# A Strassen pair's last two products moved behind the next pair's first two, with weight blocks in quarter buffers and stores on ScalarE

## The chip, the cores and the metric

The kernel runs on one core of a Trainium2 chip. The metric is the device time of one execution in microseconds (us), the median of the runs shown. TensorE (PE in the profile) multiplies into PSUM, VectorE (DVE) and ScalarE (ACT) read PSUM and work on SBUF, GpSimd (POOL) works on SBUF alone, and SyncE (SP) does nothing here but issue DMAs. Each of these engines executes its own list of instructions in order, so one that waits holds up all that stand behind it on its engine.

## The reference, cut to what matters

One decoder layer over a sequence of 2048 positions and 1024 channels, in float32:

```python
h = rms_norm(x, g_norm) * (1 + scale) + shift          # scale, shift from silu(c) @ w_mod
proj = h @ w_in                                        # (2048, 1024) @ (1024, 8192)
x_rnn, z_rnn, q, k, v, z_attn, g_r, g_a = split(proj)  # eight parts, 1024 wide each
y_rnn  = (rg_lru(conv4(x_rnn)) * silu(z_rnn)) @ w_out_rnn      # two sigmoid gates by 8 blocks 128x128
y_attn = (dilated_attention(rope(q), rope(k), v) * silu(z_attn)) @ w_out_attn
merged = sigmoid(g_r + b_r) * y_rnn + sigmoid(g_a + b_a) * y_attn
out = rms_norm(x + gate * (merged @ w_o), g_final)
```

The change concerns `proj`. All of it but the part `v` is computed by the loop that the change rearranges.

## The kernel before, in words

**Precision.** Each float32 operand is split into a high part and the rest (`hi_act` on ScalarE, then `lo_pool` on GpSimd, lines 150 to 157), and a product is three matmuls (`mm3`, line 145).

**Two halves.** The sequence is cut in four banks of 512 positions. A half (`f` = 0, 1) takes two banks. In each half `values_half` computes `v` from 256-wide weight blocks (`load_wv`, `values`), and builds the right-hand operands B11, B21 (`build_even`), B12, B22 and their sums T1 to T4 (`build_odd`): transposes on TensorE into the PSUM pool `pg`, evicted by ScalarE and VectorE. Then come 28 *pairs*: 20 in the stage of the recurrence and the gates (8 of `recurrent`, 12 of `gate_pairs`), and 8 of `qk_pairs`.

**A pair** (`strassen`, line 240) computes two 128-row blocks of `proj` (i = 0, 1) for the half's two banks (j = 0, 1) with seven products instead of eight, Strassen's scheme in Winograd's form. A product is 4 x 3 = 12 matmuls of 512 columns, so a pair is 84. Four PSUM accumulators take them, each a bank of the pool `pj`: X (B11, later B21), Z (T2), W (T3, later T4) and V (T1, later B22). Before the second product of an accumulator may start, its first contents are read out: u1 = X by ScalarE, u2 = Z + u1 (line 260) and u3 = W + u2 (line 265) by VectorE, and V + u3 for the block (1, 1) by `done`, through `total` (line 282).

**The left operands** of the seven products come from the weights. In the first half `load_raw` (line 185) fetches one pair's block of 1024 x 256 into a single buffer `wraw`, as one DMA or several; `left_operands` forms sums of its quarters a11, a12, a21, a22 on VectorE (s1 and s2 at lines 218, 219 and 226, a21 in place at line 221) in the single buffers `s1` and `s2`, and `split_s` splits each operand into one of seven buffers `S`. Each S is also stored to memory (`sD`, line 231) and in the second half `stored_operands` (line 234) fetches it back instead. All these DMAs are issued by SyncE.

**Consumers** (`done`): a recurrent pair's x blocks go through a convolution (line 530), a split (xh, xl), the two gate products into the pool `pg` (line 539) and a chain of element-wise steps to a scan (lines 540 to 553). Gates and q, k are scaled or rotated and stored.

**Order.** No order is written by hand in this part: a scheduler places every instruction of every engine by priority, which goes by the order of the program, and by when it expects its inputs. DMAs take eight completion semaphores in turn, and one waits for the DMA before it on the same semaphore where that isn't known to have landed. The attention after it, 1566 us into the span and later, is scheduled by hand and isn't touched.

Of the kernel before, what the change touches and what calls it, by code (L numbers as in the profile page):

```python
# [10 lines left out]
F32 = mybir.dt.float32  # L11
F32R = mybir.dt.float32r
BF16 = mybir.dt.bfloat16
I32 = mybir.dt.int32
AF = mybir.ActivationFunctionType
ALU = mybir.AluOpType
AX = mybir.AxisListType
PSUM = bass.MemoryType.PSUM
DRAM = bass.MemoryType.DRAM

P = 128
# [63 lines left out]
def decoder_block(ctx, tc, x, c, positions, g_norm, w_mod, b_mod, w_in, b_gate, conv_w, conv_b,  # L85
# [4 lines left out]
    def T(pool, shape, dt, tag, **kw):  # L90
        cnt[0] += 1
        return pool.tile(shape, dt, tag=tag, name=f"{tag}_{cnt[0]}", **kw)
# [57 lines left out]
    def hi_act(o, i):  # L150
        nc.scalar.activation(o, i, AF.Copy)  # L151
# [4 lines left out]
    def lo_pool(o, i, h):  # L156
        nc.gpsimd.tensor_tensor(o, i, h.bitcast(F32), ALU.subtract)  # L157
# [24 lines left out]
        nc.sync.dma_start(raw[:], src.rearrange("(k p) m -> p k m", p=P))  # L182
        return split_w(raw[:], lo)

    def load_raw(pieces):

        raw = T(wq, [P, KT, 2 * P], F32, "wraw", bufs=1)
        a = 0
        for src in pieces:
            n = src.shape[1]  # L190
            nc.sync.dma_start(raw[:, :, a : a + n], src.rearrange("(k p) m -> p k m", p=P))  # L191
            a += n
        assert a == 2 * P
        return raw

# [4 lines left out]

    def split_s(src):
        t = T(wq, [P, 2, KH, P], F32R, "S", bufs=7)
        hi_act(t[:, 0], src)
        lo_pool(t[:, 1], src, t[:, 0])
        return t

    n_pair = [0, 0]

    def left_operands(raw):

        a11, a12 = raw[:, :KH, :P], raw[:, KH:, :P]
        a21, a22 = raw[:, :KH, P:], raw[:, KH:, P:]
        yield split_s(a11)
        s1 = T(wq, [P, KH, P], F32, "s1", bufs=1)
        s2 = T(wq, [P, KH, P], F32, "s2", bufs=1)
        nc.vector.tensor_tensor(s1[:], a21, a22, ALU.add)
        nc.vector.tensor_tensor(s2[:], s1[:], a11, ALU.subtract)
        yield split_s(s2[:])  # L220
        nc.vector.tensor_tensor(a21, a11, a21, ALU.subtract)
        yield split_s(a21)
        yield split_s(s1[:])
        yield split_s(a12)
        yield split_s(a22)
        nc.vector.tensor_tensor(s2[:], a12, s2[:], ALU.subtract)
        yield split_s(s2[:])

    def first_operands(x, pieces):
        for i, t in enumerate(left_operands(load_raw(pieces))):  # L230
            nc.sync.dma_start(sD[7 * x + i], t[:].bitcast(F32))
            yield t

    def stored_operands(x):
# [5 lines left out]
    def strassen(up, f, pieces, done):  # L240

        x, n_pair[f] = n_pair[f], n_pair[f] + 1
        ops = stored_operands(x) if f else first_operands(x, pieces)

        def prod(ps, b, first, last):
            s = next(ops)
            bh, bl = B[b]
            for k in range(KH):
                mm3(ps[:], s[:, 0, k, :], s[:, 1, k, :], bh[:, k, :], bl[:, k, :],
                    first=first and k == 0, last=last and k == KH - 1, skip_group_check=True)  # L250

        X = T(pj, [P, CH], F32, "pj")
        prod(X, "B11", True, False)
        Z = T(pj, [P, CH], F32, "pj")
        prod(Z, "T2", True, True)
        u1 = T(up, [P, CH], F32, "u1", bufs=1)
        u2 = T(up, [P, CH], F32, "u2", bufs=2)
        with tc.high_priority():
            nc.scalar.activation(u1[:], X[:], AF.Copy)
            nc.vector.tensor_tensor(u2[:], Z[:], u1[:], ALU.add)  # L260
        W = T(pj, [P, CH], F32, "pj")
        prod(W, "T3", True, False)
        u3 = T(up, [P, CH], F32, "u3", bufs=1)
        with tc.high_priority():
            nc.vector.tensor_tensor(u3[:], W[:], u2[:], ALU.add)  # L265
        V = T(pj, [P, CH], F32, "pj")
        prod(V, "T1", True, False)
        done(1, 1, V, u3)
        prod(X, "B21", False, True)
        done(0, 0, X, None)  # L270
        prod(W, "T4", False, True)
        done(1, 0, W, u2)
        prod(V, "B22", False, True)
        done(0, 1, V, u2)

    def total(dst, ps, u, perm=lambda ap: ap):

# [4 lines left out]
                nc.vector.tensor_tensor(dst, perm(ps[:]), perm(u[:]), ALU.add)  # L282

    def load_wv(m):
        raw = load_raw([wcol(4 * D + m * 2 * P, 2 * P)])
        ws = []
        for k in range(0, KT, KH):
            wh = T(wq, [P, KH, 2 * P], F32R, "S", bufs=7)
            wl = T(wq, [P, KH, 2 * P], F32R, "S", bufs=7)
            hi_act(wh[:], raw[:, k : k + KH, :])  # L290
            lo_pool(wl[:], raw[:, k : k + KH, :], wh[:])
            ws.append((wh, wl))
        return ws

# [3 lines left out]
    def wcol(c0, n=P):  # L298
        return w_in[0, :, c0 : c0 + n]
# [11 lines left out]


    wq = pools.open("wq", side="right", bufs=1)
    pj = pools.open("pj", bufs=5, space=PSUM)
    pg = pools.open("pg", bufs=3, space=PSUM)
    vx = pools.open("vx", bufs=1)

    xv = x[0].rearrange("(n j r) d -> n r j d", n=NB, r=4)
# [175 lines left out]
    def reset_rows(rp, f):  # L494
        bigr = T(rp, [P, HALF], BF16, "bigr")
        for q in range(2):
            t = T(rp, [P, CH], I32, "posi", bufs=1)
            n = 2 * f + q
            nc.sync.dma_start(t[:], positions[0:1, n * CH : (n + 1) * CH].broadcast_to([P, CH]))
            nc.vector.tensor_scalar(bigr[:, q * CH : (q + 1) * CH], t[:], 0, BIG, ALU.is_equal, ALU.mult)  # L500
        return bigr

    def recurrent(rp, bigr, f, m):
        raw = T(rp, [P, 2, P], F32, "gr_", bufs=1)
        nc.sync.dma_start(raw[:, 0, :], w_a[0, m])
        nc.sync.dma_start(raw[:, 1, :], w_x[0, m])
        gh = T(rp, [P, 2, P], F32R, "gh", bufs=2)
        gl = T(rp, [P, 2, P], F32R, "gl", bufs=2)
        hi_act(gh[:], raw[:])
        lo_pool(gl[:], raw[:], gh[:])  # L510
        cw = lambda j: par[:, C_CW + 8 * j + m : C_CW + 8 * j + m + 1]
# [101 lines left out]

    def qk_pairs(qp, f, Ct, St):
        for base, dstT, qs in ((2 * D, qT, -SCALE), (3 * D, kT, 1.0)):
            def scaled(t, ps, u):
                if u is None:
                    nc.scalar.activation(t[:], ps[:], AF.Copy, scale=qs)
                else:
                    total(t[:], ps, u)  # L620
                    if qs != 1.0:
                        nc.scalar.activation(t[:], t[:], AF.Copy, scale=qs)

            def rotated(i, j, ps, u):
                n = 2 * f + j
                cq = slice(j * CH, (j + 1) * CH)
                t0 = T(qp, [P, CH], F32, "t0", bufs=3)
                t1 = T(qp, [P, CH], F32, "t1", bufs=2)
                scaled(t0, ps, u)
                nc.vector.stream_shuffle(t1[:], t0[:], swap)  # L630
                nc.gpsimd.tensor_tensor(t0[:], t0[:], Ct[:, cq], ALU.mult)
                nc.vector.tensor_tensor(t1[:], t1[:], St[:, cq], ALU.mult)
                nc.vector.tensor_tensor(t1[:], t1[:], t0[:], ALU.add)
                for hh in range(4):
                    r0 = (4 * i + hh) * P
                    nc.sync.dma_start(dstT[r0 : r0 + 32, :, n * P : (n + 1) * P],
                                      t1[hh * 32 : (hh + 1) * 32, :].rearrange("p (r j) -> p r j", r=4))

            strassen(qp, f, [wcol(base + hh * P, 32) for hh in range(H)], rotated)
            cuts = []  # L640
            for t in range(6):
                pieces = []
                i0 = t * P
                while i0 < (t + 1) * P:
                    hd, i = divmod(i0, 96)
                    n = min(96 - i, (t + 1) * P - i0)
                    pieces.append((i0 - t * P, hd * P + 32 + i, n))
                    i0 += n
                cuts.append(pieces)
            for t in range(0, 6, 2):  # L650
                def plain(i, j, ps, u):
                    n = 2 * f + j
                    t0 = T(qp, [P, CH], F32, "t0", bufs=3)
                    scaled(t0, ps, u)
                    for p0, r0, m in cuts[t + i]:
                        nc.sync.dma_start(dstT[r0 : r0 + m, :, n * P : (n + 1) * P],
                                          t0[p0 : p0 + m, :].rearrange("p (r j) -> p r j", r=4))

                strassen(qp, f, [wcol(base + r0, n) for pc in cuts[t : t + 2] for _, r0, n in pc], plain)


    def gate_pairs(ep, f):
        for m in range(0, KT, 2):
            for base, dst, b0 in ((5 * D, zaT, None), (6 * D, grT, C_BG), (7 * D, gaT, C_BG + 8)):
                def gate(i, j, ps, u):
                    n = 2 * f + j
                    t = T(ep, [P, CH], F32, "ev", bufs=3)
                    v = ps
# [33 lines left out]
    for f in range(2):  # L702
# [16 lines left out]
                next(gates, None)  # L719
        for _ in gates:  # L720
            pass
        pools.close("rp")
        qp = pools.open("qp", bufs=1)
        tabs = rotary_tables(qp, f)
# [2 lines left out]
        else:  # L727
            xp = pools.open("xp", side="right", bufs=1)
            x0 = load_x(xp, 2, "x", 2)
            norm_x(xp, x0, 1)  # L730
        qk_pairs(qp, f, *tabs)
        pools.close("qp")
    pools.close("wq", "hp", "pg", "pj")
    wp[0] = pools.open("wp", side="right", bufs=1)
# [573 lines left out]
```

## Time and profile before

| | us |
|---|---|
| median of 3 runs (2512.85 to 2521.59) | 2516.35 |
| the profiled execution, its own time | 2514.89 |
| its span, first to last instruction | 2513.1 |
| PE, DVE, ACT, POOL busy | 2306.7, 1409.9, 1174.5, 1027.6 |
| mean granted TensorE clock | 0.969 |

The profiled execution is 1.5 us below the median. In it the first half's values and builds run up to 166 us, its recurrence and gates to about 645, its rotary tables and q, k pairs to 861; the second half's values run to 980, its pairs to 1565. A group of rows has the source line, the engine, the operation, output and inputs, the shapes and the count, then busy time and mean duration, then the engine's idle time just before and what ended it. The waits are rows of the form "who waited <- for whom", total, times, longest.

### The profile page before, as it was taken

Reading aid. Unit: us, or ns where it says so; the run is one execution under the profiler, and the core shown is the slowest. Engines: PE = TensorE matmul, PEld = TensorE weight load, DVE = VectorE, ACT = ScalarE, POOL = GpSimd, SP = SyncE. Lnnn points to the kernel's source line nnn. Section 1 sums busy time; section 2 is a strip of 40 time slices with the busy share of each in tenths; the row PEclk is TensorE's granted clock in tenths of the full one; section 3 lists DMA queues with packets and bytes.
Section 4 is the critical chain, followed back from the end, with each engine's and each line's share of the span. In section 5 each row is a group of like instructions: output and inputs, shape, how many; then the busy total and the mean of one; then the engine's idle time right before and its main releaser. Section 6 shows DMA issues by size and latency. Waiting matters only on the chain.

```text
span 2513.1 us, 34056 instructions
## 1 busy us (share of the span) xinstructions
PE 2306.7 (92%) x11653; PEld 1920.7 (76%) x11653; DVE 1409.9 (56%) x2479; ACT 1174.5 (47%) x2216; POOL 1027.6 (41%) x793
## 2 busy tenths in 40 slices
PE   5898998989978889999999999899999898979998
PEld 5886776766756788888888777688878787868887
DVE  7917565656664381544435442466666767756533
ACT  2425555555522342645446110566667666633211
POOL 2547555655434452211111010466676757552100
PEclk9999999999989899999999999899999999989999
DMA  7256666666868726667666876677677677677652
GB/s 239 81 176 240 232 229 231 228 234 218 263 191 230 237 85 207 214 219 238 208 221 208 273 227 203 192 201 216 182 211 212 183 199 214 184 220 243 204 167 92
DMA packets 426181, 518.39 MB, mean 206 GB/s; under 512 B 67486, under 2 KB 310294, under 8 KB 424984
## 3 DMA queue, kind: packets, MB, share of 16 engines
q1 hardware_dynamic: 426008, 516.21, 65.1%
q8 instruction: 92, 1.51, 0.2%
q14 instruction: 81, 0.66, 0.1%
HBM read 321.07 MB, written 195.04 MB: 205 GB/s over the span
## 4 chain that ended last, share of the span: by engine, by line
PE 49%; DVE 12%; DMA 11%; issue 6%; ACT 5%; POOL 4%; SPq 3%; DVEq 0%; POOLq 0%; ACTq 0%
PE pj L143 34%; PE pq L143 7%; DMA wraw<-in_w_in_dram 5%; PE o L143 2%; PE sc L143 2%; POOL S L157 2%; PE pg L143 1%; DMA yraw<-yaT 1%; DVE wl L160 1%; ACT S L151 1%; PE pT L899 1%; ACT wh L151 1%; SPq L191 1%; PE sc L1009 1%; PE pT L919 1%
## 5 line engine op out<-in xcount | busy, mean ns | idle before, releaser
L143 PE MATMUL pj<-T,S 128*128 128x512 f32 x4704 | 1144.7, 403 | 55.9 <-DVE u L265 21.4
L143 PEld LDWEIGHTS pj<-T,S 128*128 128x128 f32 x4704 | 896.3, 192 | 289.8 <-DVE u L265 26.6
L157 POOL TENSOR_TENSOR S<-wraw,S 128x512 fp32r<-128x512 f32 (+1 forms) x140 | 229.9, 1650 | 284.7 <-ACT S L151 230.2
L143 PE MATMUL pj<-yh,wh 128*128 128x512 f32 x512 | 218.2, 427 | 18.1 <-ACT yh L151 15.9
L143 PE MATMUL pj<-yh,wl 128*128 128x512 f32 x512 | 204.7, 400 | 1.7 <-DVE wl L160 1.7
L143 PE MATMUL pj<-yl,wh 128*128 128x512 f32 x512 | 205.1, 401 | 1.1 <-POOL yl L157 1.0
L151 ACT ACTIVATE S<-wraw 128x512 fp32r<-128x512 f32 (+1 forms) x140 | 97.5, 709 | 161.1 <-DMA wraw<-in_w_in_dram 143.1
L143 PE MATMUL pj<-S,T 128*128 128x256 f32 x1152 | 158.0, 295 | 15.1 <-POOL S L157 8.0
L143 PEld LDWEIGHTS pj<-S,T 128*128 128x128 f32 x1152 | 150.1, 201 | 18.5 <-POOL S L157 9.5
L157 POOL TENSOR_TENSOR S<-s,S 128x512 fp32r<-128x512 f32 x84 | 125.6, 1495 | 71.9 <-ACT S L151 67.9
L160 DVE TENSOR_TENSOR wl<-wraw,wh 128x1024 fp32r<-128x1024 f32 x64 | 94.2, 1472 | 69.2 <-ACT wh L151 67.9
L530 DVE SCALAR_TENSOR_TENSOR xc<-xr,par,xc 128x512 f32<-128x512 f32 x96 | 93.9, 978 | 66.8 <-ACT xc L528 66.3
L143 PEld LDWEIGHTS pj<-yh,wh 128*128 128x128 f32 x512 | 98.7, 193 | 31.5 <-ACT yh L151 17.5
L519 POOL TENSOR_TENSOR zs<-zs,sg 128x512 f32<-128x512 f32 x32 | 42.5, 1328 | 182.9 <-ACT sg L518 169.4
L143 PEld LDWEIGHTS pj<-yh,wl 128*128 128x128 f32 x512 | 97.9, 191 | 24.8 <-DVE wl L160 3.1
L157 POOL TENSOR_TENSOR yl<-yraw,yh 128x512 fp32r<-128x512 f32 x40 | 57.2, 1437 | 144.3 <-ACT yh L151 136.6
L157 POOL TENSOR_TENSOR kq<-kraw,kq 128x512 fp32r<-128x512 f32 (+1 forms) x64 | 101.6, 1590 | 27.2 <-ACT kq L151 23.9
L260 DVE TENSOR_TENSOR u<-pj,u 128x512 f32<-128x512 f32 x56 | 38.5, 687 | 130.8 <-PE pj L143 125.5
L143 PEld LDWEIGHTS pj<-yl,wh 128*128 128x128 f32 x512 | 98.8, 193 | 14.4 <-POOL yl L157 3.1
L830 ACT ACTIVATE pp<-pp,st 128x128 f32<-128x128 f32 (+3 forms) x128 | 71.4, 559 | 80.8 <-DVE st L829 78.9
L143 PE MATMUL pq<-oh,mh 128*128 128x512 f32 x256 | 98.3, 396 | 5.7 <-ACT mh L151 5.7
L157 POOL TENSOR_TENSOR wh<-vraw,wh 128x640 fp32r<-128x640 f32 (+1 forms) x32 | 53.6, 1675 | 117.1 <-ACT wh L151 70.9
(292 smaller groups left out, 4426.2 us busy)
## 6 DMA issues: line engine op xcount, KB each, us to landing
sD<-S SPq DMA_DIRECT2D x196, 512.0 KB, 3.1
S<-sD SPq DMA_DIRECT2D x196, 512.0 KB, 4.4
wraw<-in_w_in_dram SPq DMA_DIRECT2D x26, 1024.0 KB, 5.7
wraw<-in_w_out_rnn_dram SPq DMA_DIRECT2D x32, 512.0 KB, 4.2
wraw<-in_w_out_attn_dram SPq DMA_DIRECT2D x32, 512.0 KB, 4.9
T<-in_w_mod_dram SPq DMA_DIRECT2D x8, 1024.0 KB, 12.4
vN<-ev SPq DMA_DIRECT2D x64, 128.0 KB, 2.7
wraw<-in_w_in_dram SPq DMA_DIRECT2D x16, 512.0 KB, 6.1
```

What stands on the lines that cost most here:

```text
L143: last_mm[0] = nc.tensor.matmul(o, lhsT=l, rhs=r, start=st, stop=sp, **kw).ins
L151: nc.scalar.activation(o, i, AF.Copy)
L157: nc.gpsimd.tensor_tensor(o, i, h.bitcast(F32), ALU.subtract)
L160: nc.vector.tensor_tensor(o, i, h.bitcast(F32), ALU.subtract)
L191: nc.sync.dma_start(raw[:, :, a : a + n], src.rearrange("(k p) m -> p k m", p=P))
L260: nc.vector.tensor_tensor(u2[:], Z[:], u1[:], ALU.add)
L519: nc.gpsimd.tensor_tensor(z[:], z[:], sg[:], ALU.mult)
L530: nc.vector.scalar_tensor_tensor(xc[:], xr[:, i : i + CH], cw(i), xc[:], ALU.mult, ALU.add)
L830: nc.scalar.activation(pdst, pdst, AF.Exp, bias=m_, scale=-1.0, accum_out=l_)
L899: nc.tensor.transpose(pt[:, c0 + j * P : c0 + (j + 1) * P], pp[i][:, k * P : (k + 1) * P], ident)
L919: nc.tensor.transpose(pt[:, (b % 2) * 2 + half, :], pp[:, half * P : (half + 1) * P], ident)
L1009: nc.tensor.transpose(pa[:, b, :], self.M[:, g, 2 * b + i : 2 * b + i + 1].broadcast_to([P, P]), ident)
```

## The change

`strassen` computes products 1 to 5 at its place and returns a function `rest` with products 6 and 7 and their evictions; the next pair calls it (`finish`) after its own products 1 and 2, and it is called where a stage ends. The operands of 6 and 7 are still prepared in their old place. `u2` gets a third buffer, and u1 is read right after product 1. `pj` has six PSUM banks instead of five, `pg` two instead of three. A pair's weights come as four tiles of 512 x 128 in five buffers, loaded in the order a11, a21, a22, a12; values' weights as tiles of 256 x 256 from the same buffers, split in pieces of two k tiles. The store of an operand is issued by ScalarE, two operands later than it was, behind that operand's high part. To make room, the recurrence's gate weights have one buffer each, and positions share one with `sg`. Closures that now run later bind their loop variables.

```diff
-    def load_raw(pieces):
-        raw = T(wq, [P, KT, 2 * P], F32, "wraw", bufs=1)
-        ...
+    NRAW = 5
+    def split_s(src):
+        t = T(wq, [P, 2, KH, P], F32R, "S", bufs=7)
+        last_hi[0] = nc.scalar.activation(t[:, 0], src, AF.Copy).ins
+        lo_pool(t[:, 1], src, t[:, 0])
+        return t
+    def blocks(pieces):
+        ...
+        def load(i, half):
+            t = T(wq, [P, KH, P], F32, "wraw", bufs=NRAW)
+            for o, src in tiles[i]:
+                nc.sync.dma_start(t[:, :, o : o + src.shape[1]],
+                                  src[half * KH * P : (half + 1) * KH * P].rearrange("(k p) m -> p k m", p=P))
+            return t[:]
+        a11, a21, a22 = load(0, 0), load(1, 0), load(1, 1)
+        return a11, load(0, 1), a21, a22
     def first_operands(x, pieces):
-        for i, t in enumerate(left_operands(load_raw(pieces))):
-            nc.sync.dma_start(sD[7 * x + i], t[:].bitcast(F32))
+        for i, t in enumerate(left_operands(pieces)):
+            kept.append((7 * x + i, t))
+            if len(kept) > 2:
+                k, t2 = kept.pop(0)
+                with tc.issue_after(last_hi[0]):
+                    nc.scalar.dma_start(sD[k], t2[:].bitcast(F32))
+            ...
             yield t
...
         prod(X, "B11", True, False)
+        u1 = T(up, [P, CH], F32, "u1", bufs=1)
+        with tc.high_priority():
+            nc.scalar.activation(u1[:], X[:], AF.Copy)
         Z = T(pj, [P, CH], F32, "pj")
         prod(Z, "T2", True, True)
-        u1 = T(up, [P, CH], F32, "u1", bufs=1)
-        u2 = T(up, [P, CH], F32, "u2", bufs=2)
+        u2 = T(up, [P, CH], F32, "u2", bufs=3)
         with tc.high_priority():
-            nc.scalar.activation(u1[:], X[:], AF.Copy)
             nc.vector.tensor_tensor(u2[:], Z[:], u1[:], ALU.add)
+        finish()
         W = T(pj, [P, CH], F32, "pj")
...
-        prod(W, "T4", False, True)
-        done(1, 0, W, u2)
-        prod(V, "B22", False, True)
-        done(0, 1, V, u2)
+        s6, s7 = next(ops), next(ops)
+        def rest():
+            prod(W, "T4", False, True, s6)
+            done(1, 0, W, u2)
+            prod(V, "B22", False, True, s7)
+            done(0, 1, V, u2)
+        open_pair.append(rest)
+    open_pair = []
+    def finish():
+        while open_pair:
+            open_pair.pop()()
...
     def load_wv(m):
...
+            for k2 in range(0, KH, 2):
+                t = T(wq, [P, 2, 2 * P], F32, "wraw", bufs=NRAW)
+                ...
+                hi_act(wh[:, k2 : k2 + 2], t[:])
+                lo_pool(wl[:, k2 : k2 + 2], t[:], wh[:, k2 : k2 + 2])
...
-    pj = pools.open("pj", bufs=5, space=PSUM)
-    pg = pools.open("pg", bufs=3, space=PSUM)
+    pj = pools.open("pj", bufs=6, space=PSUM)
+    pg = pools.open("pg", bufs=2, space=PSUM)
...
-            t = T(rp, [P, CH], I32, "posi", bufs=1)
+            t = T(rp, [P, CH], I32, "sg", bufs=1)
...
-        gh = T(rp, [P, 2, P], F32R, "gh", bufs=2)
-        gl = T(rp, [P, 2, P], F32R, "gl", bufs=2)
+        gh = T(rp, [P, 2, P], F32R, "gh", bufs=1)
+        gl = T(rp, [P, 2, P], F32R, "gl", bufs=1)
```

## The prediction

> **What bounds the kernel now.** I read the busy times first: PE 2306.7 of 2513.1 us, so what can be won is PE's idle and slowed time. I cut the span into stages next, since a mean over them hides where it lies (columns: stretch, length, busy and count of PE, PEld, DVE, ACT, POOL, granted clock, DMA share, GB/s):
>
> ```profile
> 200.00:645.00 445.00, 396.80 (x1606) 308.01 (x1605) 280.64 (x299) 264.43 (x430) 257.96 (x179) 0.97 0.66 228
> 645.00:735.00 90.00, 73.42 (x292) 55.39 (x292) 62.08 (x120) 34.30 (x60) 36.58 (x28) 0.91 0.75 228
> 735.00:860.00 125.00, 111.75 (x458) 87.23 (x457) 49.55 (x63) 33.13 (x56) 53.87 (x38) 0.96 0.81 241
> 860.00:950.00 90.00, 76.62 (x585) 73.79 (x584) 61.34 (x83) 37.61 (x60) 50.08 (x28) 0.92 0.36 109
> 950.00:1410.00 460.00, 459.52 (x2090) 375.26 (x2089) 196.22 (x261) 228.74 (x346) 78.51 (x60) 1.00 0.68 223
> ```
>
> The same pairs run in the first half (200 to 645) and in the second (950 to 1410). The second, which loads finished operands, is solid PE: 50 us hold 216 matmuls (1050 to 1100), 0.2315 each. The first would need 1606 x 0.2315 = 372 of its 445 us; 73 are lost, 48 of them idle, 25 in matmuls slowed. Beside it 28 are lost from 645 to 735 (part of the matmuls there are shorter) and 19 from 735 to 860. About 120 us is all that this change can reach. Whom PE waits for between 185 and 850 us:
>
> ```profile
> PE pj L143 <- DVE u L265: 21.4, 11, 3.0
> PE pj L143 <- ACT S L151: 14.6, 7, 6.0
> PE pg L143 <- ACT xh L151: 14.3, 11, 5.4
> PE pg L603 <- DVE rep L602: 12.2, 10, 3.9
> PE pj L143 <- DVE ev L282: 9.7, 7, 2.4
> PE pj L143 <- DVE zs L282: 5.4, 4, 2.6
> ```
>
> u, ev and zs are evictions that must be read before products 6 and 7 may add to W and V: 36.5 us. Why VectorE is late with them shows in the order of time:
>
> ```profile
> 475.35 0.69 DVE L218 TENSOR_TENSOR s<-wraw 128x512 f32<-128x512 f32 x1 [4.34 <-DMA wraw<-in_w_in_dram]
> 476.15 1.74 DVE L219 TENSOR_TENSOR s<-s,wraw 128x512 f32<-128x512 f32 x1
> 477.82 0.68 DVE L221 TENSOR_TENSOR wraw<-wraw 128x512 f32<-128x512 f32 x1
> 478.42 0.68 DVE L260 TENSOR_TENSOR u<-pj,u 128x512 f32<-128x512 f32 x1
> ...
> 481.03 0.68 DVE L265 TENSOR_TENSOR u<-pj,u 128x512 f32<-128x512 f32 x1
> 481.76 4.41 PEld L143 LDWEIGHTS pj<-T,S 128*128 128x128 f32 x13 [3.42 <-DVE u L265]
> 481.76 4.61 PE L143 MATMUL pj<-T,S 128*128 128x512 f32 x12 [2.98 <-DVE u L265]
> ```
>
> VectorE stands 4.34 us at the raw block, u2 and u3 queue behind it, PE stands 2.98 us, and then 12 matmuls take 4.61 us instead of 2.8: the clock was granted at 0.53 from 482 to 485. From 200 to 645 VectorE waits so for 81.1 us in 17 cases, ScalarE for 58.0. One buffer makes this: it is free only when operand 6 of the pair has been split, and the next load lands 5.4 us (median, 160 to 860) after its issue.
>
> **The change, part by part.** Against the profiled execution's 2514.89 us; the median is 1.5 us above.
>
> *Products 6 and 7 later.* In the order in which the changed program's instructions stand, PE goes 1, 2 (next pair), 6, 7 (old pair), 3, 4, 5. Between product 3 into W and product 6 into W stand four products instead of two, 48 x 0.2315 = 11.1 us instead of 5.6; V the same. The longest of these waits is 3.0 us, so 5.5 us more cover each: -36.5. Six banks let every bank be read out over four products, so none of this comes back as a wait for a bank. Bounds: 0 (VectorE just gets later) and -36.5.
>
> *Quarter buffers.* a11, a21 and a22 of the next pair need buffers free after operand 3, so they land about a pair ahead; a12 is used late. PE's waits for a split behind a raw load (14.6, 13.1 of them from 735 to 850) go but for the stage's start: -12, bounds 0 and -14.6. The bytes are the same; only the gates' runs get shorter, 512 B for 1024, where DMA has 0.66 of its time taken.
>
> *Clock.* Granted 0.97 over 445 us with the two levels 1 and 0.5 means 27 us at half, 13.4 lost. The waits that go are 33 of 48 idle us there: -9, bounds 0 and -13.4. The Trainium skill ("TensorE: Matmul & The Clock Gate", Part 1, What's actually happening) has the clock halved after an idle window of about 3.4 us; here it halved after 2.98 and, at 434, after 2.47. By that rule one gap of the stage alone (5.4 at 249) would count, and the sum would be 7 us higher; the trace decides.
>
> *What is late next.* The buffers s1 and s2 stay single. Operand 7 of a pair (in s2) waits for its S, free when the old product 7 is done, and only after its split may s2 take the next pair's operand 2. Product 2 of the next pair came eight products after that; now it comes four after (3, 4, 5, 1): 11.1 us. The loop is ACT 0.62, POOL 1.5, DVE 1.13, ACT 0.62, POOL 1.5 (their means from 200 to 645) = 5.4 us, on engines that are 58 to 63% busy; waiting half a service here and there it takes some 9. So it fits, barely: I take 0.3 us a pair, +8. Bounds: 0, and 1.5 us a pair, +42.
>
> *Stores on ScalarE.* 196 issues, on SP 0.32 us each:
>
> ```profile
> L231 SPq DMA_DIRECT2D sD<-S x196: 319/320/3434, 164.6 to 850.8; - x196
> ```
>
> That is 63 us of ScalarE in the first half, 2.2 a pair. ScalarE's 264.4 us from 200 to 645, over 1512/84 = 18 pairs, is 14.7 a pair; with the stores 16.9 of the 20.7 that PE would need (371.8/18), and 58.0 us of waiting for raw blocks leave it. So 0, hidden in that idle time; without the cover up to +63. Behind a waiting store stand the next split, u1 and the sigmoids, and for them wait PE and VectorE; the store waits for GpSimd's half of an operand split two operands before, and for the eighth DMA before it. Upper bound below, as a rival. SP loses 196 issues, worth nothing: nothing on the path waits for SP's time.
>
> *Values and builds.* All of a bank's weights are now ready early, and the scheduler sets 262 and 250 value matmuls ahead of most of `build_odd`'s transposes, which before stood among them. A k step of `build_odd` takes VectorE 11.5 us (897.5 to 943.3 in the second half, four steps). Two steps lie bare in the first half and three in the second, with 44 and 32 value matmuls (0.116 us each) among them. Laid out with these durations the phase ends at 170 instead of 166 and 993 instead of 980, +17, and VectorE, less disturbed by GpSimd (0.68 us for a sum that takes up to 1.8 beside it), should give half back: +8. Bounds -5 and +30. Of the prologue: SP now sets ten quarter loads, five waiting for GpSimd, ahead of six loads of `w_mod`; these are 12 to 33 us issued and used from 32.6 on, and I put the delay at 12 us, just covered: 0, up to +8 if not.
>
> *Gate products.* `pg` with two banks serves the two gates of a block, evicted 0.68 us each: 0. The second block's gate products stand 57 matmuls behind its accumulator instead of 93, 13 us for a chain of about 6: +2 (0 to +10). Waits for xh (14.3) and for the rotary rows (12.2) stay. One buffer of gate weights, the shared position tile and the closures: nothing, they are fetched or used once a pair or a half.
>
> Sum: -36.5 - 12 - 9 + 8 + 0 + 8 + 2 = -39.5, so 2475.4, and 2477 as a median.
>
> **Rivals.** *All of it comes.* The loop of s2 has its slack, the clock stays up, the builds cost nothing: -36.5 - 14.6 - 13.4 = 2450 us, 2452 as a median. For it: the second half has no such wait with the shorter cover of five banks. Against it: there ScalarE and GpSimd had no splits to do.
>
> *The waits change their name.* PE is let go by VectorE and stands before a split: the loop of s2 at 1.5 us a pair (+42 in place of +8), 2511. For it: recurrent pairs overfill engines. Their two x blocks cost VectorE about 2 x 9.5 us of lines 530 to 558, so such a pair is above the 22 us that PE takes, and the gate pairs must make up for it. Against it: 11.1 us of room.
>
> *ScalarE becomes the bound (slower).* The place is the ACT queue of the first half, the mechanism a store that holds it while it waits. 24.7 us a pair (445/18) less 14.7 busy is 10 us; seven stores fill it at 1.43 us each. From there the pair gets longer than before; at 2 us it is 28.7, 4 x 20 pairs = +80, 2595. For it: SP's store issues stood 6.42 us for three (477) and 19.5 for seven (422), which SP could afford. Against it: most of that was waiting for GpSimd just then, and the store now comes two operands later; a store lands 2.6 us after issue, the eighth DMA before it is some 10 us old. The Trainium skill ("Perfetto Trace Analysis", DMA Instruction — HWDGE) adds that issuing queues share one descriptor generator under a lock; no row of this kernel, with one queue, can show that.
>
> **How the numbers follow.** Chances: the forecast 0.55 (2455 to 2500), all of it 0.15, the change of name 0.18 (2500 to 2520), ScalarE 0.12. The range leaves out most of ScalarE and the far end of the gain, 0.2: 2435 to 2525. A measurement of this kernel can tell 0.3%, 7.5 us, from no change. Faster are the first two and under half of the third, 0.78; the rest of the third is within 0.3%, 0.09; slower 0.13.
>
> **What would show it.** From the old 200 to 645, the stage's 1606 matmuls in some 405 us; PE's waits for u L265, ev and zs under 5 us; VectorE's waits for raw blocks under 15 of 81; PE waiting for S now and then behind product 2; ScalarE near 80% busy; the values of the second half a few us longer; 1566 and later unchanged in length. Wrong if ScalarE's idle time is found ahead of DMA issues, or if PE stands long at S.

## The result, and the profile after

The changed kernel takes 2485.41 us (median of four, 2483.23 to 2487.46) where the kernel before takes 2518.40 beside it: a ratio of 0.9872 (95% interval 0.9854 to 0.9889), 33 us less. The forecast was 2477, inside 2435 to 2525. Profiled execution against profiled execution it is 2514.89 to 2487.46, -27.4 (the one after is the slowest of its four), where the sum said -39.5.

The first account is by stage, from the one profiled execution of each kernel. PE's timeline gives each boundary: the first matmul of the pairs, the end of their 1344th (sixteen pairs), the first matmul of the second half's values, the first of its pairs behind them, the end of the last pair, and PE's last matmul (us):

```
                       start of  first 16  rest to 2nd  values,  pairs,   attention, to
                       pairs     pairs     half         2nd half 2nd half PE's last
before                 166.1     395.2     300.1        118.2    585.8    939.5
after                  178.0     364.6     278.9        130.9    584.7    939.8
```

The pairs of the first half gain 51.9 us, more than the sum's -47.5 for them; the two value phases give 24.6 back (11.9 and 12.7), where the sum had 8. The rest is within 1.1 us. The stages of the changed kernel (stretch, length, busy and count of PE, PEld, DVE, ACT, POOL, granted clock, DMA share, GB/s), from the start of its pairs on, with cuts at 537.1 and at 715, behind the rotary tables:

```profile
178.00:537.10 359.10, 335.33 (x1396) 265.42 (x1395) 249.09 (x251) 224.20 (x366) 224.73 (x156) 0.97 0.71 248
537.10:715.00 177.90, 153.75 (x623) 119.68 (x622) 121.02 (x180) 92.91 (x155) 95.16 (x66) 0.94 0.72 234
715.00:821.40 106.40, 106.40 (x459) 85.55 (x458) 52.07 (x67) 34.87 (x59) 58.66 (x42) 0.99 0.92 286
821.40:952.30 130.90, 107.22 (x826) 102.63 (x825) 56.77 (x83) 47.18 (x80) 56.00 (x41) 0.90 0.33 101
```

From the start of the pairs to the second half's values PE idles 47.9 us (length less busy, first three rows) and is busy for 595.5. The same stretch of before:

```profile
166.10:861.40 695.30, 613.41 (x2478) 475.02 (x2478) 409.15 (x498) 346.43 (x575) 372.59 (x261) 0.96 0.70 232
```

That is 81.9 us idle and 613.4 busy. So of the 51.9 us 34.0 are waits and 17.9 are matmuls that run faster. The qk pairs (715 on) are solid now. In the values PE idles 23.7 us and the clock is at 0.90.

Whom PE waits for from 160 to 850 us (us in total, times, longest):

```profile
PE pg L143 <- ACT xh L151: 29.0, 11, 4.8
PE pg L644 <- DVE rep L643: 12.5, 8, 4.4
PE pj L143 <- DVE u L291: 5.5, 4, 3.9
```

u, ev and zs, 36.5 us before, are 5.5 now; the 14.6 for S are gone; but xh, PE's wait for the gate product's input, has doubled from 14.3. The timeline around one of the long ones shows why:

```profile
357.59 1.72 POOL L157 TENSOR_TENSOR S<-s,S 128x512 fp32r<-128x512 f32 x1
357.65 7.52 SPq L220 DMA_DIRECT2D wraw<-in_w_in_dram  x3
...
358.87 0.69 DVE L320 TENSOR_TENSOR zs<-pj,u 128x512 f32<-128x512 f32 x1
...
361.28 0.80 ACT L569 ACTIVATE xc<-xr,par 128x512 f32<-128x512 f32 x1
...
362.96 0.69 DVE L233 TENSOR_TENSOR s<-wraw,wraw 128x512 f32<-128x512 f32 x1 [3.41 <-POOL S L157]
363.69 1.63 DVE L236 TENSOR_TENSOR wraw<-wraw,wraw 128x512 f32<-128x512 f32 x1
365.25 2.31 DVE L571 SCALAR_TENSOR_TENSOR xc<-xr,par,xc 128x512 f32<-128x512 f32 x3
367.60 0.63 ACT L151 ACTIVATE xh<-xc 128x512 fp32r<-128x512 f32 x1 [4.42 <-DVE xc L571]
368.28 1.22 PE L143 MATMUL pg<-xh,gh 128*128 128x512 f32 x2 [4.75 <-ACT xh L151]
```

VectorE stands 3.41 us at L233, the next pair's s1, and the convolution, whose input was ready at 362.08, is queued behind it until 365.25. The row names GpSimd; but s1's own buffer had been free since GpSimd's split that ended at 359.31 (the first row), and L233 also needs the raw quarters a21 and a22, whose issues stand on SP from 357.65 on. So I read it as the picture of before (raw6 below tests it): VectorE at a raw block, with another instruction behind it. VectorE's waits at its operands, before from 200 to 645 and now from 190 to 620 us:

```profile
DVE s L218 <- DMA wraw<-in_w_in_dram: 81.1, 17, 10.0
```

```profile
DVE s L233 <- DMA wraw<-in_w_in_dram: 35.5, 9, 6.0
DVE s L234 <- POOL S L157: 25.7, 14, 2.7
DVE s L241 <- POOL S L157: 21.6, 11, 2.7
```

### The profile page after: what moved, and what is told of

Its sections match the earlier page's. It is cut to its first block, busy times and chain, and to the rows that moved or that the text cites. A ratio compares the mean times of both kernels' runs of the same rounds, so it can differ in the third digit from the quotient of the medians.

```text
span 2485.6 us, 34395 instructions
## 1 busy us (share of the span) xinstructions
PE 2293.6 (92%) x11653; PEld 1915.6 (77%) x11653; DVE 1408.2 (57%) x2479; ACT 1179.7 (47%) x2242; POOL 1038.8 (42%) x821
## 4 chain that ended last, share of the span: by engine, by line
PE 55%; DMA 6%; DVE 6%; issue 3%; ACT 2%; POOL 1%; SPq 1%; ACTq 0%; POOLq 0%; DVEq 0%
PE pj L143 38%; PE pq L143 7%; PE o L143 3%; PE sc L143 3%; DMA vraw<-vN 1%; DMA wraw<-in_w_out_attn_dram 1%; PE pT L942 1%; PE pg L143 1%; DVE wl L160 1%; ACT wh L151 1%; DMA yraw<-yaT 1%; PE pT L962 1%; PE sc L1052 1%; DMA fg<-mrT 0%; DMA meT<-fg 0%
## 5 line engine op out<-in xcount | busy, mean ns | idle before, releaser
L143 PE MATMUL pj<-T,S 128*128 128x512 f32 x4704 | 1123.3, 398 | 6.3 <-DVE u L291 5.5
L157 POOL TENSOR_TENSOR S<-wraw,S 128x512 fp32r<-128x512 f32 x168 | 234.0, 1405 | 158.7 <-ACT S L196 65.1
L143 PEld LDWEIGHTS pj<-yh,wl 128*128 128x128 f32 x512 | 98.3, 192 | 25.7 <-DVE wl L160 3.9
L284 DVE TENSOR_TENSOR u<-pj,u 128x512 f32<-128x512 f32 x56 | 38.4, 685 | 118.6 <-PE pj L143 72.2
L143 PE MATMUL pq<-ol,mh 128*128 128x512 f32 x256 | 101.0, 394 | 0.0
L143 PE MATMUL pq<-oh,ml 128*128 128x512 f32 x256 | 100.0, 392 | 0.0
```

What stands on the lines that cost most here:

```text
L143: last_mm[0] = nc.tensor.matmul(o, lhsT=l, rhs=r, start=st, stop=sp, **kw).ins
```

## The experiments

Each is an edit of the changed kernel. The same stages (us, one profiled execution each), and the time:

```
                       start of  first 16  rest to 2nd  values,  time, median     ratio to before
                       pairs     pairs     half         2nd half                  (95% interval)
in_order               178.8     363.2     277.2        128.4    2481.0           0.9854 (0.9834-0.9874)
whole_raw              165.7     382.8     288.4        129.8    2499.5           0.9928 (0.9911-0.9945)
neither                168.0     405.5     288.2        131.1    2521.3           1.0026 (1.0012-1.0039)
stores_sp              177.7     365.2     281.5        131.9    2489.4           0.9887 (0.9866-0.9907)
stores_now             177.0     369.9     279.8        128.7    2492.2           0.9909 (0.9894-0.9924)
s2_two                 178.7     367.6     279.3        128.6    2492.6           0.9908 (0.9894-0.9923)
raw6                   179.4     353.7     270.7        129.9    2467.5           0.9802 (0.9785-0.9819)
build_early            164.7     364.4     281.8        110.9    2453.6           0.9760 (0.9743-0.9777)
raw6_early             166.3     353.1     272.4        114.9    2442.9           0.9703 (0.9688-0.9718)
raw6_early_inorder     166.3     364.6     270.8        112.0    2448.4           0.9727 (0.9711-0.9743)
raw7_early_inorder     166.3     362.9     274.1        110.5    2446.7           0.9723 (0.9707-0.9739)
best                   165.9     352.6     272.7        113.5    2443.6           0.9711 (0.9696-0.9726)
```

**in_order.** Products 6 and 7 back in their place.

```
-        open_pair.append(rest)
+        rest()
```

> The changed kernel with products 6 and 7 put back ahead of the next pair's product 1 (quarter buffers, stores by ScalarE and six pj banks stay). If the later place of the two products made the gain of the first half's pairs, PE's waits for u, ev and zs come back to 25 us or more (36.5 before the change, 5.5 after it) and the pairs of the first half get 25 to 35 us longer: 2510 to 2520. If the quarter buffers made it, because VectorE no longer stands at a raw block, these waits stay under 10 us and the time under 2493.

The second branch. It is no slower than the changed kernel (2481.0, 2485.4; the intervals overlap), and the first sixteen pairs take 363.2 us for 364.6. PE's waits from 180 to 850 us:

```profile
PE pg L143 <- ACT xh L151: 12.8, 7, 3.5
PE pg L644 <- DVE rep L643: 11.4, 9, 3.9
PE pj L143 <- DVE u L291: 10.8, 3, 3.7
PE pj L143 <- DVE ev L320: 2.7, 7, 0.6
```

u and ev come back to 13.5 us, xh falls by 16.2. With five quarter buffers the later place only moves the wait from the one to the other.

**whole_raw** and **neither.** Raw weights of pairs and values whole again, in the one buffer of before, with the products late and, in neither, in their old place as well.

```
-        a11, a12, a21, a22 = blocks(pieces)
+        raw = load_raw(pieces)
...
-            for k2 in range(0, KH, 2):
...
+        raw = load_raw([wcol(4 * D + m * 2 * P, 2 * P)])
```

> The changed kernel with the raw weights of pairs and values loaded whole into one buffer again, as before the change (products 6 and 7 late, stores by ScalarE, six pj banks stay). If the later place alone covers VectorE's lateness, the waits for u, ev and zs stay under 8 us; VectorE's waits for raw blocks go back to some 80 us, the operand waits of the qk pairs return (14.6 us), and the values, whose weights come late again, lie among the transposes as before: start of the pairs back from 178 to 166-170 and values of the second half from 131 to some 118 us, together 20 to 24 us less. Sum 2485 - 22 + 15 + 0 to 15 for xh: 2478 to 2493. If the quarter buffers are what keeps VectorE on time, the u, ev and zs waits return too: over 2500. If the longer values are not due to the early weights, they stay at 178 and 131: over 2500 as well, told apart by the stage.

> The changed kernel with whole raw buffers again and products 6 and 7 in their old place: only the six pj banks, the two pg banks, u2's third buffer and the stores by ScalarE are left of the change. If the other two parts made all the gain of the pairs, PE's waits for u, ev and zs are back above 25 us and the first 28 products' worth of pairs (1344 matmuls) take 385 to 395 us as before the change: 2510 to 2525. If banks or stores gave some of it: under 380 and under 2505.

PE from 180 to 850 us in whole_raw, and from 165 to 850 in neither:

```profile
PE pg L143 <- ACT xh L151: 41.7, 16, 4.3
...
PE pj L143 <- DVE u L281: 3.4, 3, 1.6
```

```profile
PE pj L143 <- DVE u L281: 34.2, 8, 6.9
PE pg L143 <- ACT xh L151: 17.4, 9, 2.7
PE pj L143 <- DVE ev L310: 14.9, 10, 2.9
```

(The 1344 matmuls of the second expectation are sixteen pairs, not 28 products.) With whole buffers the later place does what the prediction said of it: u and ev go from 49.1 to 3.4. But VectorE is as late as ever:

```profile
DVE s L223 <- DMA wraw<-in_w_in_dram: 89.0, 18, 7.8
```

(whole_raw, 190 to 620), and half of the gain comes back at the next instruction that needs VectorE: xh rises from 17.4 to 41.7. The sixteen pairs gain 22.7 us (405.5 to 382.8) by the later place alone, 42.3 by the quarter buffers alone (363.2), and 40.9 by both (364.6). Banks and stores by ScalarE without the other two bring nothing (1.0026; in neither the sixteen pairs take 10 us more than before the change, the rest of the half 12 less). In the sizes, whole_raw was expected at 2478 to 2493 and took 2499.5: xh, and the second half's values, which stayed at 129.8 (2 of them nine matmuls of the first pair, set among the values). PE's waits for S came back as expected, 13.1 us in three rows. In the first half the pairs do start at 165.7 again. So the 12 us there come with the early value weights; the 12 in the second half do not come with them alone.

**stores_sp** and **stores_now.** The stores by SP; and by ScalarE, but straight behind the split.

```
-            kept.append((7 * x + i, t))
-            ...
+            nc.sync.dma_start(sD[7 * x + i], t[:].bitcast(F32))      # stores_sp
+            nc.scalar.dma_start(sD[7 * x + i], t[:].bitcast(F32))    # stores_now
```

> The changed kernel with the 196 operand stores issued by SP again, straight after the split. If they are hidden on either queue: within 3 us of 2485. If SP, standing at a store for GpSimd's half, holds the raw loads queued behind it, VectorE's waits for raw blocks (35.5 us in nine cases from 190 to 620) rise above 60 and the time goes to 2495 or more. If ScalarE pays for the stores, its queue frees and the time falls by 5 us or more.

> The changed kernel with each store issued on ScalarE straight after its operand's split instead of two operands later. ScalarE then stands at 196 stores for GpSimd's half of the same operand, about 1.5 us each beside 0.3: seven a pair is 10 to 13 us, more than the 5 us a pair that are left of ScalarE's 18 us. If ScalarE's queue can become the bound as the prediction's rival has it: pairs of the first half longer by 1 to 4 us each, 2510 to 2570, with xh and u named by PE. If there is slack enough: within 8 us of 2485.

The store queue is worth little: stores_sp is 4 us slower with an overlapping interval of the ratio, and VectorE's waits for raw blocks did not rise (28.0 us, for 35.5). In the changed kernel the row of the line that issues the stores shows no idle time ahead of them, and durations of

```profile
L251 ACTq DMA_DIRECT2D sD<-S x194: 326/326/872, 169.4 to 805.4; - x194
```

0.33 us each (shortest, median, longest in ns). In stores_now ScalarE does stand for GpSimd's half. From 190 to 620 us, whichever of its instructions comes behind the waiting store has the wait in its row:

```profile
ACT S L196 <- POOL S L157: 43.1, 23, 2.6
...
ACT sg L552 <- POOL S L157: 13.2, 7, 2.0
...
ACT ev L711 <- POOL S L157: 7.0, 6, 1.3
ACT L584 <- POOL S L157: 5.3, 7, 0.8
```

With two smaller rows these are 72.2 us in 47 cases, where the changed kernel has none. Yet the sixteen pairs take 5.3 us more, not the 16 to 64 that I expected. ScalarE's waits for VectorE fall in the same stretch from 148.5 to 66.2 us: most of the new standing took the place of old standing, and PE felt little of it (xh 32.6 for 29.0).

**s2_two** and **raw6.** Which of VectorE's two waits counts: the one for s2 at L234 and L241 (25.7 and 21.6 us), or the one for raw quarters at L233 (35.5)?

```
-        s2 = T(wq, [P, KH, P], F32, "s2", bufs=1)            # s2_two
+        s2 = T(wq, [P, KH, P], F32, "s2", bufs=2)
-        nc.vector.tensor_tensor(s2[:], a12, s2[:], ALU.subtract)
+        s7 = T(wq, [P, KH, P], F32, "s2", bufs=2)
+        nc.vector.tensor_tensor(s7[:], a12, s2[:], ALU.subtract)
...
-    NRAW = 5                                                  # raw6
+    NRAW = 6
-            t = T(ev, [P, 2, 256], F32, "ev", bufs=2)         # both, for the room
+            t = T(ev, [P, 2, 256], F32, "ev", bufs=1)
```

> The changed kernel with a sixth quarter buffer (its room taken from the values' second eviction buffer). Theory: PE's 29.0 us at the gate products (ACT xh, four of about 4.8 us, each followed by slowed matmuls) come from VectorE, which stands 3.4 us at the next pair's raw quarters (L233) with the convolution xc queued behind; a buffer more lets these loads start earlier: VectorE's waits at L233 from 39 to under 15 us, xh from 29 to under 14, time down by 12 to 25 us to 2460-2473. Rival: VectorE is held by the single s2 (L234 and L241 wait 47 us for GpSimd's splits); then xh stays over 22 and the time within 5 us of 2485.

> The changed kernel with two buffers of s2, operand 7 in one of its own (the room comes from the values' second eviction buffer; five quarter buffers stay). VectorE's waits for GpSimd at L234 and L241, 25.7 and 21.6 us from 190 to 620, go to under 8 together. If they hold the convolution back, PE's waits for xh fall from 29 to under 15 and the time by 10 to 20 us. If VectorE has the room and only the raw quarters matter, as the kernel with six quarter buffers says, where these two waits stayed at 56 us, PE's waits stay and the time is within 5 us of 2485.

raw6 is 17.9 us faster. PE from 180 to 850, then VectorE from 190 to 620:

```profile
PE pg L143 <- ACT xh L151: 17.6, 8, 3.5
...
PE pj L143 <- DVE u L291: 5.8, 5, 3.6
```

```profile
DVE s L234 <- POOL S L157: 35.9, 15, 3.8
DVE s L241 <- POOL S L157: 20.4, 11, 2.1
...
DVE s L233 <- DMA wraw<-in_w_in_dram: 9.1, 3, 3.5
```

The raw wait falls to 9.1, the waits for s2 grow to 56.3, and the kernel is faster: VectorE has the room for these. In s2_two the wait at L234 is gone, the one at L241 (there L242) stays at 20.6, against the expectation, and the raw one is up,

```profile
DVE s L233 <- DMA wraw<-in_w_in_dram: 56.8, 8, 9.3
```

xh stands at 33.1, and it is 7 us slower. Ahead of these loads SP no longer stands for L234 (59.9 us in the changed kernel, 190 to 620), but longer for GpSimd's splits (177.9 us for 125.1); why was not taken apart.

**build_early.** The odd bank's transposes ahead of three of the even bank's four value blocks.

```
-        for m in range(4):
-            ws = load_wv(m)
-            values(vx, m, ws, n0)
-        norm_x(vx, xs)
-        build_odd(vx, xs)
+        ws = load_wv(0)
+        values(vx, 0, ws, n0)
+        norm_x(vx, xs)
+        build_odd(vx, xs)
+        for m in range(1, 4):
+            ws = load_wv(m)
+            values(vx, m, ws, n0)
```

> The changed kernel with the odd bank's norm and build_odd written after the first of the even bank's four value blocks instead of after all four. If the longer value phases (start of the pairs 166 to 178 us, values of the second half 118 to 131 us) come from the order, 262 and 250 value matmuls ahead of the transposes that VectorE must then do with little beside them, the phases get 10 to 15 and 15 to 25 us shorter: 2448 to 2462. If they come from the value weights' 56 short splits or from late loads, the order changes nothing: within 5 us of 2485.

2453.6, 31.9 less. The second half's values:

```profile
811.00:921.80 110.80, 101.25 (x826) 98.68 (x825) 62.63 (x83) 45.80 (x80) 60.43 (x41) 0.98 0.39 119
```

PE's idle time there falls from 23.7 to 9.6 us and the clock rises from 0.90 to 0.98; both value phases are shorter than before the change. The short splits are all still there, so it is the order: in the second half the longest run of value matmuls between two groups of transposes falls from 250 to 68.

**raw6_early**, **raw6_early_inorder**, **raw7_early_inorder**, **best.** The two gains together; products 6 and 7 back on top; a seventh quarter on top of that; and the first with the values' second eviction buffer given back, its room from build_odd, where two differences are made in place, with three buffers of hf:

```
-            tt(t[0][:], h1[:], f32("B11", 0, k), ALU.subtract)
+            tt(t2[:], h2[:], h1[:], ALU.subtract)
+            tt(h1[:], h1[:], f32("B11", 0, k), ALU.subtract)
...
```

> The changed kernel with both edits that gained: a sixth quarter buffer and the odd bank's build ahead. They act in different stages (pairs of the first half; value phases), so if the accounts are right they add: 2485.4 - 17.9 - 31.9 = 2436, within 5 us. If the time won in one stage is lost in the next (loads that come earlier colliding with the values' stores), it is over 2445.

> The same with products 6 and 7 back in their old place. With five quarter buffers the old place was 4.4 us faster (2481.0 to 2485.4), with xh at 12.8 us for 29.0. If the later place costs by itself (the two evictions of the old pair fall among the convolution's VectorE work of the next), the gain comes again: 2430 to 2434. If six buffers have given VectorE room, the two are equal within 3 us; if the cover of four products is worth something once nothing else is late, this is 4 us or more slower.

> The same with a seventh quarter buffer (room from two differences of build_odd made in place, and from u2's third buffer, which the old order does not need). VectorE waited 9.1 us for raw blocks with six buffers and later products, 15.5 with five in the old order. If raw loads still hold it, 3 to 8 us faster than six; if not, within 3 us, with build_odd's in-place form neutral.

> The kernel with six quarter buffers, late products and the early build, with the values' second eviction buffer given back (its room comes from two differences of build_odd made in place). That kernel missed its sum by 7 us (2442.9 for 2436); its values of the second half took 114.9 us where the kernel with the early build alone took 110.9. If the single eviction buffer is the cause, they go back to 111 and the time falls to 2436-2440. If it is not, the time stays at 2443 within 3 us; if six quarter buffers themselves take the value phases longer, likewise.

raw6_early is the fastest shown, 0.9703 of before, but 7 us short of its sum. best looked for these in the eviction buffer: 2443.6, values 113.5. It was not the cause, so the single eviction buffer of raw6 costs nothing that these runs tell either, and the 7 us stay open. With six quarters the later place pays a little: 353.1 for 364.6 us in the sixteen pairs, 2440.3 to 2443.9 against 2445.6 to 2452.0 in time (the intervals of the ratio just touch); a third branch of the expectation, and the opposite of in_order. PE from 165 to 850 us, later place (raw6_early) and old place (raw6_early_inorder):

```profile
PE pg L143 <- ACT xh L151: 15.6, 7, 3.5
...
PE pj L143 <- DVE u L291: 5.0, 5, 2.8
```

```profile
PE pj L143 <- DVE u L291: 17.4, 5, 4.1
...
PE pg L143 <- ACT xh L151: 4.9, 5, 2.4
```

A seventh quarter changes nothing.

## Why the prediction was right, and where it was not

*Products 6 and 7 later, -36.5.* The waits went (-31.0; the 5.5 left are just over the 5 of the sign), so the number nearly holds, but the step fails in its cause. "VectorE just gets later", the bound at 0, was the answer for the later place as built here: beside five quarter buffers it is worth nothing (in_order). I had priced VectorE's lateness at u, ev and zs only. It is removed by the quarters, which let VectorE start on time; covered at the evictions alone, it reappears at xh.

*Quarter buffers, -12.* The operand waits are gone as said. The step is mis-sized because it counted PE's waits for S alone: the quarters shorten VectorE's stand at raw blocks, from 81.1 us in 445 to 35.5 in 430, and so carry the first step's 31 us as well: in_order, with the quarters alone, gains as much as both. The sign "under 15" was wrong, and the 35.5 left cost the 17.9 us that raw6 gains.

*Clock, -9.* The total came out, but not where the term had it. Summed over the records of the granted clock, the time lost from the start of the pairs to the second half's values was 30.7 us and is 22.2. In the stage that the term was worked out for it only went from 15.4 to 11.9 (200 to 645 before, the same 1606 matmuls from 206.1 to 624.8 now); the qk pairs, 5.1 to 0.6, gave the larger part. That is luck in the sum: in that stage fewer gaps were left, but those at xh are longer. PE's busy time fell by 17.9 us, more than any term had. Matmuls ran at the half clock for 51.9 us before and for 32.2 now, which is 9.9 us of it. Most of the rest goes with the number of gaps, 60 before and 29 now: a matmul behind a gap takes 0.50 us where matmuls in a run follow each other at 0.2315, and the runs between gaps (those without rotary or transpose work) were together 15.1 us longer than their count at 0.2315 and full clock, and are 7.6. In the changed kernel the clock was at half after every gap of 3.8 us or more in these stages (two matmuls 1.22 us at 368.28, against 0.73 to 0.74 after gaps of 1.15). In the kernel before, eight of the 14 gaps of 2.04 to 2.98 us in these stages were followed by the half clock and six, up to 2.96, were not; a drop lasted 3.41 us or a multiple. The Trainium skill's window of about 3.4 us ("TensorE: Matmul & The Clock Gate", Part 1, What's actually happening) agrees with these gaps; the shorter ones of before that halved it (2.47 and 2.98 us) speak against it as a lower bound.

*Late next, +8.* Nothing: PE waits for no S of a pair at all. VectorE stands for the loop of s2 for 47.3 us, and raw6 shows that it has room for more; s2_two, which took away about half of it, gained nothing.

*Stores, 0.* Right. ScalarE from 178 to 537 is busy 224.2 us and issues 111 stores of 0.33: 73% of the time, for the 80% named. The rival in which it becomes the bound is shown wrong even without the delay of two operands. (The 2.6 us after which it has a store land is the shortest in before; the median was 3.1 and is 3.8 now.)

*Values and builds, +8.* The term that cost the forecast most: +24.6. I had laid out +17 and halved it on the thought that VectorE would run freer; no row said so. The order I named was the cause: build_early takes all of it back and more. For the second half I had put that order down to the early weights, and whole_raw, without them, is as long; the instructions of neither and whole_raw stand in another order there than those of before, with two pg banks in place of three. It is not the changed kernel's order either: the longest run of value matmuls among the transposes is 98 there, for 250. No run tried the bank alone, so why those two are as long stays open.

*Gate products, +2.* +14.7. I looked at the second block, whose distance shrinks from 93 to 57 matmuls. The four longest waits (4.6 to 4.8) are at the first block, as at 368.28, whose distance is about 44 before and after; not the distance changed there but VectorE's queue.

So the total held by luck in its largest terms: the 36.5 us credited to the later place were made by the quarter buffers, priced at 12, and the two together came out. The rest is 12 us short in profiled time (-27.4 for -39.5): the pairs gained 51.9 for 47.5, the values lost 24.6 for 8. The stage of 1606 matmuls that was to take 405 us took 419 (206.1 to 624.8). "The waits change their name" came about in part, by another path: 14.7 us at xh, not at S.

## What to carry to other kernels

Ask what makes an engine late before covering its lateness: distance put between a late eviction and its reader moves the wait to the next reader of the same engine, while an earlier load removes it, and then the distance can pay too (here some 5 us, with six buffers). A change that makes operands ready earlier also lets a scheduler move work ahead of what feeds another engine; price the order that it then chooses at full, stage by stage. And of two waits on an engine the longer total (s2, 56 us in raw6) may be the harmless one; take each away once before believing either. A trace puts a wait into the row of the next instruction of the engine: sum the rows by what they waited for, not by who waited.

## What was not expected of the hardware

A store that ScalarE issued straight behind its split, before GpSimd's half was ready, cost the kernel 7 us for 196 of them (stores_now), though ScalarE stood 72 us in 430 for GpSimd: on an engine that was busy 63% of the time, these waits took the place of 82 us of waits for VectorE.
